# The inverse root mean square of a state-space group: one power on GpSimd in place of Newton steps on VectorE

## The chip, the cores and the metric

The kernel runs on one core of a Trainium2 chip. The metric is device time in microseconds, the median of several runs; lower is better. The engines are TensorE (PE in the profile, PEld its weight loads), VectorE (DVE), ScalarE (ACT), GpSimd (POOL) and SyncE (SP, which issues DMAs). Each engine works through its own queue in order, and semaphores hold it where it needs another engine's result.

## The reference

Two layers of a decoder trunk on 512 tokens of width 1024, in float32. A layer is a half-step SwiGLU feed-forward block, a mixer and a second half-step feed-forward block, each behind a root-mean-square normalization. The mixer has two branches, stick-breaking attention (4 heads) and a Mamba-2 state-space scan (24 heads in 8 groups), merged by gates. What the change touches is the end of the state-space branch, the normalization of each group of 192 channels:

```python
y = y.reshape(b, s, SSM_D_INNER) * jax.nn.silu(z.astype(jnp.float32))
yg = y.reshape(b, s, SSM_GROUPS, SSM_D_INNER // SSM_GROUPS)
yg = yg * lax.rsqrt(jnp.mean(yg * yg, axis=-1, keepdims=True) + NORM_EPS)
return (yg.reshape(b, s, SSM_D_INNER) * ssm_norm.astype(jnp.float32)).astype(z.dtype)
```

## The kernel before

Activations are held transposed, channels on partitions and 512 tokens along the free axis. Dense products are done in three matmuls per block of 128 rows: weights and activations are each split into a high part of reduced precision and a low part, and high x high, high x low and low x high are summed (`mm3`, lines 315 to 317). Every weight block comes from memory through `wraw`, ScalarE makes the high part (`whi`, line 282) and VectorE the low one (`wlo`, line 284).

The order of all queues is written out by the program itself. The dense products are the backbone. Everything else is a side task, a Python generator that is put on a list (`spawn`) and advanced by one step at each tick; a tick comes after each three matmuls of the backbone (`dense` calls `tick`), and `yield n` lets a task rest for n ticks. So a number after `yield` decides how many steps of the backbone stand ahead of the task's next instructions in each queue; it is no time and no wait.

In the mixer the backbone is the input projection, and three kinds of side tasks run beside it:

- `conv_block`: the causal convolution of one projected block of 128 channels. ScalarE applies the first tap (line 1024), VectorE three more (line 1027), ScalarE the tanh (line 1032), VectorE the product (line 1039), and for x and B blocks TensorE transposes the result (line 853, into `pt`).
- `ssd_group`: the scan of one group over four chunks of 128 tokens, one group after the other (`ssd_on`). GpSimd weights the inputs (lines 1137, 1139), masks the decay (1145) and forms products (1147, 1179, 1184); ScalarE forms the decays and, per chunk, the sum of squares of the gated output (line 1189, into a column of `ss`). When the four sums are there, the group is normalized: `ss`, 128 tokens x 4 chunks, is scaled and shifted (line 1209), `rsqrt_small` writes the inverse root to `rstd` (tile `gny`), VectorE multiplies the first 128 channels by it (line 1219), ScalarE the remaining 64 (line 1221, four instructions into `acc`), and TensorE transposes them back some ticks later.
- attention and the gates, which are not touched.

`rsqrt_small` starts from the bit trick (line 491: the bits of the number, as an integer, times -0.5, plus a constant) and refines it by three Newton steps of three instructions each (lines 493 to 495), all on VectorE and all on 128x4.

Of the kernel before, what the change touches and what calls it, by code (L numbers as in the profile page):

```python
# [8 lines left out]
F32 = mybir.dt.float32  # L9
F32R = mybir.dt.float32r  # L10
I32 = mybir.dt.int32
AF = mybir.ActivationFunctionType
ALU = mybir.AluOpType
# [4 lines left out]
P = 128  # L18
SEQ = 512
NT = SEQ // P  # L20
# [9 lines left out]
GW = HPG * HD  # L30
# [6 lines left out]
EPS = 1e-6  # L37
# [126 lines left out]
class Builder:  # L164
# [298 lines left out]
    def consts(self):  # L463
        nc = self.nc
        c = self.cst
        self.ident = c.tile([P, P], F32, name="ident")
        make_identity(nc, self.ident)
        self.ones = c.tile([P, P], F32, name="ones")
        nc.vector.memset(self.ones, 1.0)
        self.eps = c.tile([P, 1], F32, name="eps")  # L470
        nc.vector.memset(self.eps, EPS)
        self.nones = c.tile([P, P], F32R, name="nones")
        self.ntri = c.tile([P, P], F32R, name="ntri")
        with self.tc.tile_pool(name="cst_tmp", bufs=1, reuse_waits="tile") as tp:
            neg = tp.tile([P, P], F32, name="neg")
            nc.vector.memset(neg, -1.0)
            nc.vector.tensor_copy(self.nones, neg)
            tri = tp.tile([P, P], F32, name="tri")
            nc.gpsimd.affine_select(out=tri, in_=neg, pattern=[[-1, P]], compare_op=ALU.is_ge, fill=0.0,
                                    base=0, channel_multiplier=1)  # L480
            nc.vector.tensor_copy(self.ntri, tri)
        self.upto = c.tile([P, P], F32, name="upto")
        nc.gpsimd.affine_select(out=self.upto, in_=self.ones, pattern=[[1, P]], compare_op=ALU.is_ge, fill=0.0,
                                base=0, channel_multiplier=-1)


    def rsqrt_small(self, v, y):

        eng = self.nc.vector
        t = self.t(self.mp, v.shape, "gnt", bufs=1)  # L490
        eng.tensor_scalar(y.bitcast(I32), v.bitcast(I32), -0.5, 1597463007.0, op0=ALU.mult, op1=ALU.add)
        for _ in range(3):
            eng.scalar_tensor_tensor(t, y, -0.5, v, op0=ALU.mult, op1=ALU.mult)
            eng.tensor_tensor(t, t, y, op=ALU.mult)
            eng.scalar_tensor_tensor(y, t, 1.5, y, op0=ALU.add, op1=ALU.mult)

    def norm_start(self):
        self.h, self.diff = [None] * KB, [None] * KB
# [605 lines left out]
    def ssd_group(self, layer, g):  # L1104
        nc, mp, tok = self.nc, self.mp, None
# [9 lines left out]
        y = self.t(mp, [P, NT, GW], "y", bufs=1)  # L1115
        ss = self.t(mp, [P, NT], "ss")
# [89 lines left out]
            yield 1  # L1206
        self.give("xs")
        yield 1
        nc.vector.tensor_scalar(ss, ss, 1.0 / GW, EPS, op0=ALU.mult, op1=ALU.add)
        rstd = self.t(mp, [P, NT], "gny")  # L1210
        self.rsqrt_small(ss, rstd)
        yield 2
        if g % 2 == 0:
            self.tail = self.t(self.nrm, [P, NT, P], "acc")
        tail = self.tail
# [319 lines left out]
```

## Time and profile before

| | |
|---|---|
| median of three runs | 2582.1 us (2581.85 to 2583.41) |
| the profiled execution, its own time | 2582.94 us |
| its span, first to last instruction | 2581.2 us |
| granted TensorE clock | 0.999 |
| TensorE busy | 2559.8 us |
| VectorE busy | 1752.4 us |
| ScalarE busy | 1282.0 us |
| GpSimd busy | 498.5 us |
| each of the eleven instructions on 128x4 | 0.16 to 0.20 us, 16 times or 48 times |

A row of a table of groups reads: line, engine, operation, written tile <- read tiles, shape, count, then busy time in us and mean in ns of one, then the engine's idle time before it and who ended it. A row of the table of waits reads: engine, tile and line that waited <- engine, tile and line that ended the wait: us in total, times, longest. A row of a timeline reads: start, length, engine, line, operation, tiles, shapes, count and, in brackets, the idle time before it with its releaser. A row about one line or tile gives the shortest, median and longest duration in ns and the first and last start. The chain of waits follows the work that ended last, each piece with start and length.

### The profile page before, as it was taken

Reading aid. Unit: us, or ns where it says so; the run is one execution under the profiler, and the core shown is the slowest. Engines: PE = TensorE matmul, PEld = TensorE weight load, DVE = VectorE, ACT = ScalarE, POOL = GpSimd, SP = SyncE. Lnnn points to the kernel's source line nnn. Section 1 sums busy time; section 2 is a strip of 40 time slices with the busy share of each in tenths; the row PEclk is TensorE's granted clock in tenths of the full one; section 3 lists DMA queues with packets and bytes.
Section 4 is the critical chain, followed back from the end, with each engine's and each line's share of the span. In section 5 each row is a group of like instructions: output and inputs, shape, how many; then the busy total and the mean of one; then the engine's idle time right before and its main releaser. Section 6 shows DMA issues by size and latency. Waiting matters only on the chain.

```text
span 2581.2 us, 38169 instructions
## 1 busy us (share of the span) xinstructions
PE 2559.8 (99%) x15028; PEld 2288.4 (89%) x15028; DVE 1752.4 (68%) x2426; ACT 1282.0 (50%) x2103; POOL 498.5 (19%) x614
## 2 busy tenths in 40 slices
PE   9999999999999999999999999999999999999998
PEld 7898988888888889899998989888888888899997
DVE  8575875676664478586885858756676644876766
ACT  6343556665554255343653535566555533543444
POOL 0121201143341002121121312012333310022120
PEclk9999999999999999999999999999999999999999
DMA  6454542233333454545364545423333334455452
GB/s 183 138 159 136 132 138 87 99 103 110 101 105 107 139 162 139 164 139 164 106 180 139 156 141 136 139 72 111 99 103 104 116 109 143 152 143 168 142 162 78
DMA packets 104659, 335.76 MB, mean 130 GB/s; under 512 B 11872, under 2 KB 15392, under 8 KB 104480
## 3 DMA queue, kind: packets, MB, share of 16 engines
q1 hardware_dynamic: 92672, 292.84, 34.2%
q0 software_dynamic: 10944, 39.85, 8.6%
q8 instruction: 118, 1.93, 0.3%
q10 hardware_dynamic: 864, 0.64, 0.1%
q14 instruction: 61, 0.50, 0.1%
HBM read 320.60 MB, written 12.68 MB: 129 GB/s over the span
## 4 chain that ended last, share of the span: by engine, by line
PE 93%; DVE 4%; ACT 2%; issue 1%; DMA 0%; POOL 0%; SPq 0%; DVEq 0%; ACTq 0%
PE mm L315 26%; PE mm L317 25%; PE mm L316 25%; PE pa L316 3%; PE pa L317 3%; PE pa L315 3%; PE pa L1169 2%; DVE wlo L284 1%; PE pa L1171 1%; PE pt L853 1%; PE pt L1154 1%; DVE cv L1027 1%; PE pt L1152 1%; ACT whi L282 1%; PE pa L453 0%
## 5 line engine op out<-in xcount | busy, mean ns | idle before, releaser
L282 ACT CAST whi<-wraw 128x1024 fp32r<-128x1024 f32 (+3 forms) x440 | 435.1, 989 | 584.9 <-PE mm L317 485.0
L284 DVE TENSOR_TENSOR wlo<-wraw,whi 128x1024 fp32r<-128x1024 f32 (+3 forms) x440 | 538.7, 1224 | 165.9 <-ACT whi L282 164.5
L315 PE MATMUL mm<-hhi,whi 128*128 128x512 f32 (+1 forms) x1584 | 565.1, 357 | 0.0
L317 PE MATMUL mm<-hlo,whi 128*128 128x512 f32 (+1 forms) x1584 | 554.1, 350 | 0.4 <-DVE hlo L507 0.4
L316 PE MATMUL mm<-hhi,wlo 128*128 128x512 f32 (+1 forms) x1584 | 553.0, 349 | 0.0
L317 PEld LDWEIGHTS mm<-hlo,whi 128*128 128x128 f32 x1584 | 299.9, 189 | 40.3 <-DVE hlo L507 0.8
L316 PEld LDWEIGHTS mm<-hhi,wlo 128*128 128x128 f32 x1584 | 300.4, 190 | 34.6 <-DVE wlo L284 0.2
L315 PEld LDWEIGHTS mm<-hhi,whi 128*128 128x128 f32 x1584 | 300.3, 190 | 34.2 <-ACT hhi L505 0.4
L284 DVE TENSOR_TENSOR wlo<-s,whi 128x1024 fp32r<-128x1024 f32 x152 | 235.2, 1561 | 60.4 <-ACT whi L282 60.4
L315 PE MATMUL mm<-act,whi 128*128 128x512 f32 (+1 forms) x710 | 274.2, 386 | 0.0
L317 PE MATMUL mm<-act,whi 128*128 128x512 f32 (+1 forms) x710 | 274.2, 386 | 0.0
L316 PE MATMUL mm<-act,wlo 128*128 128x512 f32 (+1 forms) x710 | 274.1, 386 | 0.0
L315 PE MATMUL mm<-th,whi 128*128 128x256 f32 x912 | 257.4, 282 | 0.0
L317 PE MATMUL mm<-tl,whi 128*128 128x256 f32 x912 | 257.0, 282 | 0.0
L316 PE MATMUL mm<-th,wlo 128*128 128x256 f32 x912 | 256.9, 282 | 0.0
L626 POOL TENSOR_TENSOR g<-g,rs 128x512 f32<-128x512 f32 x76 | 132.5, 1744 | 553.4 <-DVE g L633 534.3
L282 ACT CAST whi<-s 128x1024 fp32r<-128x1024 f32 x152 | 159.3, 1048 | 102.4 <-PE mm L317 60.7
L652 DVE SCALAR_TENSOR_TENSOR x<-mm,x 128x512 f32<-128x512 f32 x93 | 64.1, 689 | 196.0 <-PE mm L317 196.0
L254 POOL DMA_DIRECT2D s<-in_wflat_dram x76 | 65.6, 863 | 621.3 <-DMA s<-in_wflat_dram 332.4
L315 PEld LDWEIGHTS mm<-th,whi 128*128 128x128 f32 x912 | 172.4, 189 | 0.0
L316 PEld LDWEIGHTS mm<-th,wlo 128*128 128x128 f32 x912 | 172.0, 189 | 0.0
L317 PEld LDWEIGHTS mm<-tl,whi 128*128 128x128 f32 x912 | 171.9, 188 | 0.0
(306 smaller groups left out, 5088.9 us busy)
## 6 DMA issues: line engine op xcount, KB each, us to landing
wraw<-in_wflat_dram SPq DMA_DIRECT2D x328, 512.0 KB, 3.6
s<-in_wflat_dram SPq DMA_DIRECT2D x76, 512.0 KB, 4.7
s<-in_wflat_dram POOLq DMA_DIRECT2D x76, 512.0 KB, 7.4
wraw<-in_wflat_dram SPq DMA_DIRECT2D x88, 384.0 KB, 3.1
cumb<-cum_d SPq DMA_DIRECT2D x16, 768.0 KB, 4.8
xd<-x SPq DMA_DIRECT2D x16, 256.0 KB, 3.2
wraw<-in_wflat_dram SPq DMA_DIRECT2D x16, 256.0 KB, 3.6
x<-xd SPq DMA_DIRECT2D x16, 256.0 KB, 3.9
```

The lines of the kernel that those rows point to most:

```text
L254: self.nc.gpsimd.dma_start(raw, src, accum_op=ALU.add)
L282: nc.scalar.copy(hi[:, :n], raw[:, :n])
L284: nc.vector.tensor_tensor(lo[:, :n], raw[:, :n], hi[:, :n].bitcast(F32), op=ALU.subtract)
L315: mm(ps, a[0], b[0], start=start, stop=False, **kw)
L316: mm(ps, a[1], b[0], start=False, stop=False, **kw)
L317: mm(ps, a[0], b[1], start=False, stop=stop, **kw)
L626: eng.tensor_tensor(r, r, self.rs[:, cols].unsqueeze(1).to_broadcast([P, 2, half]), op=ALU.mult)
L652: self.nc.vector.scalar_tensor_tensor(x, pd, 0.5, x, op0=ALU.mult, op1=ALU.add)
L853: self.nc.tensor.transpose(pt[:, cs], src[:, cs], self.ident)
L1027: nc.vector.scalar_tensor_tensor(u[:, j:], ps[:, :SEQ - j], tap[KCONV - 1 - j], u[:, j:], op0=ALU.mult, op1=ALU.add)
L1152: nc.tensor.matmul(pc[:, :P], bt[:, span(c)], ct[:, span(c)], start=True, stop=True)
L1169: nc.tensor.matmul(py[:, i * HD:(i + 1) * HD], decs[c][:, i, :], xdts[c][:, i, :], start=True, stop=True)
```

## The change

The scale and shift of `ss` moves from VectorE to GpSimd. The inverse root is one GpSimd instruction, `ss` to the power of a constant tile that holds -0.5. The bit trick and the Newton steps go, with their temporary tile. The task then rests three ticks and not two. The constant's memset is added at the start, in a tile shared with `eps`. Lines after line 487 are eight less in the changed kernel.

```diff
-        self.eps = c.tile([P, 1], F32, name="eps")
+        small = c.tile([P, 1 + NT], F32, name="small")
+        self.eps, self.root = small[:, :1], small[:, 1:]
         nc.vector.memset(self.eps, EPS)
+        nc.vector.memset(self.root, -0.5)
...
-    def rsqrt_small(self, v, y):
-
-        eng = self.nc.vector
-        t = self.t(self.mp, v.shape, "gnt", bufs=1)
-        eng.tensor_scalar(y.bitcast(I32), v.bitcast(I32), -0.5, 1597463007.0, op0=ALU.mult, op1=ALU.add)
-        for _ in range(3):
-            eng.scalar_tensor_tensor(t, y, -0.5, v, op0=ALU.mult, op1=ALU.mult)
-            eng.tensor_tensor(t, t, y, op=ALU.mult)
-            eng.scalar_tensor_tensor(y, t, 1.5, y, op0=ALU.add, op1=ALU.mult)
...
         self.give("xs")
         yield 1
-        nc.vector.tensor_scalar(ss, ss, 1.0 / GW, EPS, op0=ALU.mult, op1=ALU.add)
         rstd = self.t(mp, [P, NT], "gny")
-        self.rsqrt_small(ss, rstd)
-        yield 2
+        nc.gpsimd.tensor_scalar(ss, ss, 1.0 / GW, EPS, op0=ALU.mult, op1=ALU.add)
+        nc.gpsimd.tensor_tensor(rstd, ss, self.root, op=ALU.pow)
+        yield 3
```

VectorE's queue at the end of group 2 of the first layer, before (`cv_5856` is a convolution block, `wlo` a low weight part, `raw_5896` the normalized group):

```order
L1027 SCALAR_TENSOR_TENSOR cv_5856<-mm_5790,conv_4136,cv_5856 128x511
L284 TENSOR_TENSOR wlo_5859<-wraw_5718,whi_5858 128x1024
L1209 TENSOR_SCALAR ss_5589<-ss_5589 128x4
L491 TENSOR_SCALAR gny_5875<-ss_5589 128x4
...
L495 SCALAR_TENSOR_TENSOR gny_5875<-gnt_5876,gny_5875 128x4
L1027 SCALAR_TENSOR_TENSOR cv_5856<-mm_5790,conv_4136,cv_5856 128x510
L1027 SCALAR_TENSOR_TENSOR cv_5856<-mm_5790,conv_4136,cv_5856 128x509
L1219 TENSOR_TENSOR raw_5896<-y_5588,gny_5875 128x512
L1039 SCALAR_TENSOR_TENSOR cv_5856<-raw_5855,cv_5856 128x512
```

And the same place of the changed kernel:

```order
L1019 SCALAR_TENSOR_TENSOR cv_5837<-mm_5771,conv_4137,cv_5837 128x511
L284 TENSOR_TENSOR wlo_5840<-wraw_5699,whi_5839 128x1024
L1019 SCALAR_TENSOR_TENSOR cv_5837<-mm_5771,conv_4137,cv_5837 128x510
L1019 SCALAR_TENSOR_TENSOR cv_5837<-mm_5771,conv_4137,cv_5837 128x509
L1211 TENSOR_TENSOR raw_5870<-y_5569,gny_5855 128x512
L1031 SCALAR_TENSOR_TENSOR cv_5837<-raw_5836,cv_5837 128x512
```

The eleven instructions between the weight part and the second tap are gone; the normalization still stands ahead of the convolution's product.

GpSimd's queue at the same place of the changed kernel (`xw` and `xdt` are the next group's weighted inputs):

```order
L1171 TENSOR_TENSOR y_5569<-y_5569,t_969_5823 128x192
L1176 TENSOR_TENSOR y_5569<-y_5569,z_5781 128x192
L1202 TENSOR_SCALAR ss_5570<-ss_5570 128x4
L1203 TENSOR_TENSOR gny_5855<-ss_5570,small 128x4
L1129 TENSOR_TENSOR xw_6034<-xs_5563,sq_4398 128x192
L1131 TENSOR_TENSOR xdt_6036<-xs_5563,sq_4398 128x192
```

Before, the product (now line 1176) was followed at once by the next group's `xw`; the two new instructions stand between them. ScalarE's queue is the same at this place, with the four scalings by `gny` ahead of the convolution's tanh:

```order
L282 CAST whi_5839<-wraw_5699 128x1024
L1181 ACTIVATE t_976_5845,ss_5570<-y_5569 128x192
L1213 ACTIVATE acc_5869<-y_5569,gny_5855 128x64 x4
L1024 ACTIVATE raw_5836<-cv_5837 128x512
L1016 ACTIVATE cv_5888<-mm_5830,conv_4137 128x512
```

TensorE's matmuls are the same in number; some transposes of normalized groups and first products of groups stand one step of the backbone (three matmuls) later.

## The prediction

> **What bounds the kernel now.** I read the busy shares first, then what TensorE waits for, then the chain of waits around those waits.
>
> ```profile
> PE 2559.8 (99%) x15028; PEld 2288.4 (89%) x15028; DVE 1752.4 (68%) x2426; ACT 1282.0 (50%) x2103; POOL 498.5 (19%) x614
> PE pt L853 <- DVE cv L1039: 4.7, 8, 0.8
> PE pt L853 <- DVE cv L1039: 1.6, 3, 0.5
> PE pt L853 <- DVE cv L1039: 0.8, 1, 0.8
> PE pt L853 <- DVE cv L1039: 0.7, 1, 0.7
> ACT acc L1221 <- DVE gny L495: 18.0, 6, 3.0
> ```
>
> TensorE is busy for 2559.8 of 2581.2 us, so only a wait of TensorE can be won; the 29 us of VectorE work that the change removes are worth nothing by themselves. The second row is its longest entry in the table of waits: eight times the transposes of line 853 wait for the convolution's last step. The third is that table for 600 to 775 us alone: three of the eight lie there, and the same row comes out, 1.6 us and three times, for 1880 to 2055 us. The last says that six times ScalarE's scaling of the tail (line 1221) waits 3.0 us for the end of the Newton chain: in groups 2, 4 and 6 of both layers, and these are the six places where TensorE stalls. The other two of the eight are the fourth and fifth row, the table for 505 to 510 us and for 1784 to 1790 us (the same place of the second layer, 1279 us later, as 1880 is to 601). No group has come to its root there: the first normalization starts at 538.6 us (row of line 1219 below). They stay.
>
> The chain of waits between 595 and 612 us, group 2 of the first layer (start, length, what):
>
> ```profile
> 600.76 0.66 issue
> 601.42 1.04 ACT whi L282
> 602.48 1.23 DVE wlo L284
> 603.71 0.09 DVE ss L1209
> 603.82 0.18 DVE gny L491
> 604.03 0.17 DVE gnt L493
> ...
> 605.60 0.16 DVE gny L495
> 605.76 0.67 DVE cv L1027
> 606.46 0.76 DVE cv L1027
> 607.25 0.04 issue
> 607.30 0.64 ACT raw L1032
> 607.96 0.70 DVE cv L1039
> 608.67 0.04 issue
> 608.71 0.66 PE pt L853 x4
> ```
>
> All eleven small instructions, 603.71 to 605.76 us, stand on the path to the transposes, and nothing in the convolution needs them: they only stand in front of its second and third tap in VectorE's queue. What the stall costs is read from TensorE's timeline there:
>
> ```profile
> 607.56 0.39 PE L316 MATMUL mm<-hhi,wlo 128*128 128x512 f32 x1
> 607.79 0.39 PE L317 MATMUL mm<-hlo,whi 128*128 128x512 f32 x1
> 608.71 0.66 PE L853 MATMUL pt<-ident,cv 128*128 128x128 f32 x4 [0.53 <-DVE cv L1039]
> ```
>
> Matmuls follow each other at 0.23 us; the transposes start 0.92 us after the last one. So 0.69 us is lost, and without a wait they would start at 608.02.
>
> **The change, part by part.** Removed from VectorE in each of 16 groups: the scale and shift (line 1209), the bit trick (491) and nine Newton steps.
>
> ```profile
> L495 DVE SCALAR_TENSOR_TENSOR gny<-gnt,gny 128x4 f32<-128x4 f32 x48 | 7.8, 163 | 1.6
> L1209 DVE TENSOR_SCALAR ss<-ss 128x4 f32<-128x4 f32 x16 | 3.2, 198 | 6.6 <-ACT t L1189 6.6
> ```
>
> Eleven instructions at about 0.16 us and one start each 0.2 us make 2.1 us (603.63 to 605.76), and 29 us of busy time in 16 groups (11 x 0.163 x 16). Of that only the part that TensorE sees counts. In group 2 the convolution's two taps would follow wlo at once, 603.71 + 0.67 + 0.76 = 605.14, against 607.22 now. From there 0.64 (line 1032) and 0.70 (1039) give about 606.6 at the transposes, which are due at 608.02: a spare 1.4 us, if nothing else holds them.
>
> Something else can: ScalarE's order is unchanged, so the four tail scalings (1.07 us) still stand ahead of the tanh of line 1032, and they need the power.
>
> ```profile
> 602.62 0.19 ACT L1189 ACTIVATION_READ_ACCUMULATOR t<-y 128x1 f32 x1
> 605.80 1.07 ACT L1221 ACTIVATE acc<-y,gny 128x64 f32<-128x64 f32 x4 [2.99 <-DVE gny L495]
> 607.30 0.63 ACT L1032 ACTIVATE raw<-cv 128x512 f32<-128x512 f32 x1 [0.43 <-DVE cv L1027]
> ```
>
> Added on GpSimd: a scale and shift, and a power, each on 128x4. If the power is written at X, the transposes can start at X + 1.07 + 0.63 + 0.70 and some 0.15 for four hand-overs, X + 2.55. So X up to 605.47 gives the whole 0.69 us, X of 606.16 gives nothing, and later ones cost 1 us for each us. The multiplication of line 1219 needs the power as well, and the convolution's last step stands behind it in VectorE's queue; it takes 0.68 us and runs beside the tails and the tanh, so it is never the later of the two.
>
> When can GpSimd begin? The sum of squares is complete at 602.81. GpSimd is then idle: its last product ended at 600.72 and its next instruction came at 610.11.
>
> ```profile
> 595.71 1.23 DVE L284 TENSOR_TENSOR wlo<-wraw,whi 128x1024 fp32r<-128x1024 f32 x1
> 595.89 1.50 POOL L1184 TENSOR_TENSOR y<-y,z 128x192 f32<-128x192 f32 x1
> 600.12 0.60 POOL L1184 TENSOR_TENSOR y<-y,z 128x192 f32<-128x192 f32 x1
> 610.11 1.06 POOL L1137 TENSOR_TENSOR xw<-xs,sq 128x192 f32<-128x192 f32 x1 [9.39 <-ACT xs L1053]
> ```
>
> But the same product takes 1.50 instead of 0.60 us where VectorE forms wlo beside it, as if it stood still until that ended. In group 2 wlo runs from 602.48 to 603.71. So I let GpSimd start at 603.71 and not at 602.85. The Trainium skill says so too (GPSIMD Engine Reference, section 8, Key points): GpSimd shares its SBUF interfaces with VectorE, in contention with VectorE instructions that have two SBUF inputs, as wlo's subtraction has. By that rule the power has 0.86 us less room than without it, and the pair of rows above agrees.
>
> What two such instructions cost, no row shows. The nearest:
>
> ```profile
> L1139 POOL TENSOR_TENSOR xdt<-xs,sq x64: 506/512/1228, 511.0 to 2073.9; 128x192 f32<-128x192 f32 x64
> L626 POOL TENSOR_TENSOR c<-c,rs x38: 1280/1281/1292, 88.1 to 2529.7; 128x512 f32<-128x512 f32 x38
> L626 DVE TENSOR_TENSOR g<-g,rs x38: 691/691/693, 91.1 to 2532.5; 128x512 f32<-128x512 f32 x38
> ```
>
> GpSimd's binary operation takes 0.51 us on 192 columns and 1.28 on 512: 2.4 ns a column and some 0.05 us. At four columns that is 0.06 us; I take 0.2 for the scale and shift, a little over what VectorE needs. The power, D, has 0.2 us as its lower bound. Its upper bound is ten arithmetic steps, as many as the chain that it replaces, each at the 0.51 us of the 192-column operation: 5.1 us. I take 0.8. The chain's 2 us on VectorE are almost all fixed cost, paid ten times for four columns; inside one instruction that is paid once, and ten steps of 2.4 ns on four columns are 0.1 us. A logarithm and an exponential may need several times as many. So X = 603.71 + 0.2 + 0.8 = 604.7, which is 0.76 us ahead of the limit. The whole gain holds up to D = 1.55, break-even is D = 2.25.
>
> The Trainium skill speaks against the step (GPSIMD Engine Reference, section 4.1, Engine selection): elementwise arithmetic belongs on VectorE, GpSimd is about two times slower. The last two rows, 1.28 against 0.69 us for the same shape, agree. By that rule the two instructions would cost twice two of VectorE's, about 0.65 us: still less than the eleven, and the sum stays.
>
> Sum: 6 x 0.69 = 4.1 us off the path.
>
> At nothing I put the following. Groups 0, 1, 3, 5 and 7 show no wait of TensorE now. In group 0 the power stands ahead of the next group's products in GpSimd's queue, which now start at 535.55, while the operation behind them waits until 541.68 for ScalarE; some 5 us of cover.
>
> ```profile
> 535.55 0.51 POOL L1137 TENSOR_TENSOR xw<-xs,sq 128x192 f32<-128x192 f32 x1
> 541.68 0.52 POOL L1145 TENSOR_SCALAR_AFFINE_SELECT dec<-dec 128x384 f32<-128x384 f32 x1 [5.15 <-ACT dec L1143]
> L1219 DVE TENSOR_TENSOR raw<-y,gny x16: 680/685/693, 538.6 to 2088.4; 128x512 f32<-128x512 f32 x16
> 543.46 0.44 PE pa L853 x4
> ```
>
> In other groups GpSimd waits for data there, as in the row at 610.11. The wait of three ticks instead of two puts the normalization one step (three matmuls, 0.68 us) later in the queues, and a few transposes with it; TensorE's number of matmuls is the same, and in group 0 the transposes (543.46) come 4 us after their operand is ready (538.6 + 0.69), as the last two rows show. Were this cover gone, it would cost what a late power costs, below. The extra memset at the start lies beside the first loads.
>
> The profiled execution took 2582.94 us (span 2581.2 and 1.7 around it); less 4.1 it is 2578.8. It lies 0.8 over the median of the runs, 2582.1, which gives 2578.0. After that the places at 507 and 1786 us, where attention and the first blocks fill VectorE, are the only waits of this kind left.
>
> **Rivals.** What a measurement of this kernel can tell from no change is about 0.2%, 5.2 us; the whole of the forecast lies inside that.
>
> A: the wait changes its owner. With D between 1.55 and 3.1 the tails wait for GpSimd as they now wait for VectorE: at D = 1.9 half the gain is left (2580), at 2.25 nothing (2582), at 3.1 six times 0.85 is lost (2587). For it: the tails wait 3.0 us today and the power has only 0.76 us to spare. Against it: four columns are little for any engine.
>
> B, slower: the power is computed in software, step by step, and D is over 3.1. Then ScalarE stands at the tails with the tanh, the next tap and the next weight block behind it, and TensorE's transposes wait in the six groups. At the upper bound, 5.1, X is 609.0, the transposes start at 611.56 instead of 608.71, and six times 2.85 makes 17 us: 2599. It decides from D = 3.1 on. For it: no row shows a power on this engine. Against it: the price per column in the rows.
>
> C: the stalls go and the time falls by more than 5.2 us. The six waits give 4.1 and the next two are out of reach, so this needs another microsecond, from the spread of the runs (2581.85 to 2583.41 now) or from the shifted order: about 2576.5.
>
> D: the stalls stay, because the first taps or the weight block in front (601.42 to 603.71) hold them. Then 2582. The 1.4 us of room counted above speak against it.
>
> **Chances.** Forecast, within 0.2%: 0.53. A: 0.13. B: 0.18. C: 0.12. D: 0.04. So faster by over 0.2% is 0.12, slower 0.18, the same 0.70. The time is that of the forecast, 2578. The range goes from 2576.5 to 2590: it leaves out half of C and the part of B with D over 3.6, some 0.06 and 0.13.
>
> **What would show it.** Right: the row of line 853 waiting for the convolution (853 and 1039 here) falls from eight times to two; the chain of waits runs on TensorE through these places; the power's row has a mean under 1.5 us; VectorE's busy time falls by some 29 us. Wrong: a power of several microseconds, ScalarE's tail waiting for GpSimd by more than 3 us, and TensorE still waiting six times for the convolution; or new waits of TensorE at groups 0, 1, 3, 5 or 7.

## The result and the profile after

The changed kernel takes 2577.65 us (2577.19 to 2579.32, 20 runs), the kernel before 2582.1 us (2581.73 to 2583.89, 20 runs): 4.45 us less, a ratio of 0.9982 with a 95% interval of 0.9976 to 0.9988. That is within the 0.2% that the prediction counts as the same, though a ratio of 1 lies outside the interval, and 0.35 us from the predicted 2578.0.

Busy shares of the changed kernel, then its longest waits of TensorE and one of ScalarE from the tables of waits:

```profile
PE 2558.2 (99%) x15028; PEld 2288.4 (89%) x15028; DVE 1724.0 (67%) x2251; ACT 1280.6 (50%) x2103; POOL 522.1 (20%) x646
PE pt L845 <- DVE cv L1031: 1.5, 2, 0.8
PE pa L958 <- DVE y L408: 1.3, 4, 0.5
ACT acc L1213 <- POOL gny L1203: 12.5, 6, 2.1
```

VectorE does 28.4 us less, GpSimd 23.6 us more. TensorE waits for the convolution twice where it waited eight times. ScalarE still waits six times for the root, now of GpSimd and 2.1 us each in place of 3.0; TensorE does not wait behind it.

The two new instructions, from the rows of their tile and line (shortest, median and longest in ns):

```profile
L1203 POOL TENSOR_TENSOR gny<-ss,small x16: 1017/1017/1043, 535.7 to 2081.3; 128x4 f32<-128x4 f32 x16
L1202 POOL TENSOR_SCALAR ss<-ss x16: 192/194/870, 535.4 to 2081.0; 128x4 f32<-128x4 f32 x16
```

And group 2 of the first layer, from the timelines of VectorE, ScalarE, GpSimd and TensorE:

```profile
601.70 1.23 DVE L284 TENSOR_TENSOR wlo<-wraw,whi 128x1024 fp32r<-128x1024 f32 x1 [0.18 <-ACT whi L282]
602.84 1.53 DVE L1019 SCALAR_TENSOR_TENSOR cv<-mm,conv,cv 128x510 f32<-128x510 f32 x2
604.28 0.68 DVE L1211 TENSOR_TENSOR raw<-y,gny 128x512 f32<-128x512 f32 x1
605.73 0.69 DVE L1031 SCALAR_TENSOR_TENSOR cv<-raw,cv 128x512 f32<-128x512 f32 x1 [0.76 <-ACT raw L1024]
...
601.83 0.19 ACT L1181 ACTIVATION_READ_ACCUMULATOR t<-y 128x1 f32 x1
604.11 1.07 ACT L1213 ACTIVATE acc<-y,gny 128x64 f32<-128x64 f32 x4 [2.09 <-POOL gny L1203]
605.08 0.62 ACT L1024 ACTIVATE raw<-cv 128x512 f32<-128x512 f32 x1
...
602.11 0.87 POOL L1202 TENSOR_SCALAR ss<-ss 128x4 f32<-128x4 f32 x1 [2.17 <-ACT t L1181]
603.06 1.02 POOL L1203 TENSOR_TENSOR gny<-ss,small 128x4 f32<-128x4 f32 x1
...
607.00 0.39 PE L317 MATMUL mm<-hlo,whi 128*128 128x512 f32 x1
607.23 0.60 PE L845 MATMUL pt<-ident,cv 128*128 128x128 f32 x4
607.59 0.47 PE L315 MATMUL mm<-hhi,whi 128*128 128x512 f32 x1
```

The two taps follow the weight part at once (602.84). The transposes start 0.23 us after the matmul before them, without a wait, and their operand is ready at 606.42, so 0.81 us of room is left. The chain between power and transposes is the one that limits it now: power to 604.08, scalings to 605.18, tanh to 605.70, last step to 606.42.

Where the time went: laid beside each other matmul by matmul (15028 in both traces), the kernel before falls behind by 0.74 to 0.77 us at each of the six places, about 4.5 us together. The rest of the difference between the two profiled spans, 5.2 us, is some 0.8 us of the first 30 us; the start varies that much without a change of the kernel (below, e11).

### The profile page after: what moved, and what is told of

Read it like the earlier page. It is cut to its first block, busy times and chain, and to the rows that moved or that the text cites. A ratio compares the mean times of both kernels' runs of the same rounds, so it can differ in the third digit from the quotient of the medians.

```text
span 2576.0 us, 38026 instructions
## 1 busy us (share of the span) xinstructions
PE 2558.2 (99%) x15028; PEld 2288.4 (89%) x15028; DVE 1724.0 (67%) x2251; ACT 1280.6 (50%) x2103; POOL 522.1 (20%) x646
## 4 chain that ended last, share of the span: by engine, by line
PE 94%; DVE 3%; ACT 2%; issue 0%; DMA 0%; POOL 0%; SPq 0%; DVEq 0%; ACTq 0%
PE mm L315 26%; PE mm L317 26%; PE mm L316 26%; PE pa L316 3%; PE pa L317 3%; PE pa L315 3%; PE pa L1161 2%; DVE wlo L284 1%; PE pa L1163 1%; PE pt L1146 1%; PE pt L845 1%; PE pt L1144 1%; PE pa L845 0%; PE pa L453 0%; PE pa L960 0%
```

## The experiments

**Is it the engine or the later place?** The change does two things: it takes the root off VectorE, and it lets the task rest three ticks, which moves normalizations and transposes in the queues. Each was done alone. TensorE's instructions stand in the first run as in the changed kernel, in the second as in the kernel before.

```diff
 # e1, from the kernel before
         self.rsqrt_small(ss, rstd)
-        yield 2
+        yield 3
 # e2, from the changed kernel
         nc.gpsimd.tensor_tensor(rstd, ss, self.root, op=ALU.pow)
-        yield 3
+        yield 2
```

> The kernel before with the rest of three ticks alone; the root stays on VectorE, and the matmuls stand in the order of the changed kernel. Theory (the gain is six waits of TensorE, which end because the eleven instructions no longer stand ahead of the convolution's taps in VectorE's queue): nothing gained, 2582.1 within 1 us, eight waits for the convolution. Rival (the later place of the normalization makes the gain): 2577.7 and two waits.

> The changed kernel with the rest of two ticks again; the power stays on GpSimd, and the matmuls stand in the order of the kernel before. Theory: the whole gain, 2577.7 within 1 us, two waits for the convolution. Rival (the later place makes it): 2582.

Measured: e1 2582.16 us against 2582.35 for the kernel before on the same chip, ratio 1.0 (0.9991 to 1.0009); e2 2577.74, ratio 0.9982 (0.9973 to 0.9991). The waits of TensorE in e1 and then in e2:

```profile
PE pt L853 <- DVE cv L1039: 4.7, 8, 0.7
```

```profile
PE pt L845 <- DVE cv L1031: 1.5, 2, 0.8
```

The whole gain comes with the engine, none with the tick; the third tick is not needed.

**Is it the length of VectorE's chain, or what replaces it?** In e3 nothing goes to GpSimd; two of three Newton steps are left out, so the root is less exact.

```diff
 # e3, from the kernel before
-        for _ in range(3):
+        for _ in range(1):
```

> The kernel before with one Newton step in place of three: two steps are left out, and the root is less exact. VectorE's chain is 6 x 0.197 = 1.18 us shorter in each group; nothing goes to GpSimd. Theory: 1.18 is more than the 0.69 of each wait, so the six waits end and the time is that of the changed kernel, 2577.9 within 1 us, with VectorE's busy time 16 us lower. Rival (what VectorE saves counts in proportion, 96 of 176 instructions): 2579.7. Rival (it takes GpSimd's power): 2582.

Measured: 2577.65 us, ratio 0.9982 (0.9974 to 0.9991), two waits for the convolution, VectorE busy 1737.8 us:

```profile
PE 2558.0 (99%) x15028; PEld 2288.6 (89%) x15028; DVE 1737.8 (67%) x2330; ACT 1282.4 (50%) x2103; POOL 496.1 (19%) x614
```

VectorE saves half of what the change saves, and the time falls by the same amount. So a wait is paid, not work: 1.18 us less ahead of the taps brings as much as the whole 2.1. How little would do was not tried; by the prediction's sum it is the 0.69 of the wait.

**How late may the power be?** One and then three more powers ahead of the one that is used; their results are not used.

```diff
 # e4 with range(1), e5 with range(3), from the changed kernel
         nc.gpsimd.tensor_scalar(ss, ss, 1.0 / GW, EPS, op0=ALU.mult, op1=ALU.add)
+        spare = self.t(mp, [P, NT], "gnt", bufs=1)
+        for _ in range(1):
+            nc.gpsimd.tensor_tensor(spare, ss, self.root, op=ALU.pow)
         nc.gpsimd.tensor_tensor(rstd, ss, self.root, op=ALU.pow)
```

> The changed kernel with one more power of 1.02 us ahead of the one that is used. In the changed kernel the operand of the transposes is ready at 606.42 us and they start at 607.39, so 0.97 us of room. Theory: the second power takes 1.05 with its start, so 0.1 us of wait in six groups, 2578.3. By the break-even of the prediction (power's length 2.25; here 2.07) half a microsecond of each wait would be back, 2581. Rival (the gain is the earlier root): all of it lost, 2582 or more.

> The changed kernel with three more powers ahead of the one that is used: the root comes 3.05 us later than in the changed kernel (a power takes 1.02). Theory (past its room of 0.77 us, which the run with two powers shows, a late power costs TensorE as much as it is late, in the six groups): 6 x 2.3 = 14 us, and up to 2 x 2.3 more in group 1 of each layer, where that run shows a first wait: 2591 to 2597, slower than before. By the break-even of the prediction (2.25, then 1 us for each us in six groups): 2593. Rival (the waits are taken up by the slack of other queues): 2582 or less.

Measured: e4 2580.53 us, ratio 0.9992 (0.9983 to 1.0001): by the medians nearly two thirds of the gain lost. e5 2603.45 us, ratio 1.0085 (1.0069 to 1.01): 21 us slower than before. From e4's chain of waits in group 2 and its timeline of TensorE:

```profile
603.87 0.88 POOL ss L1202
...
604.82 1.02 POOL gnt L1205
605.84 1.00 POOL gny L1206
...
607.12 0.81 ACT acc L1216 x3
607.93 0.53 ACT raw L1024
...
608.48 0.70 DVE cv L1031
```

```profile
608.77 0.39 PE L317 MATMUL mm<-hlo,whi 128*128 128x512 f32 x1
609.23 0.66 PE L845 MATMUL pt<-ident,cv 128*128 128x128 f32 x4
```

The powers now stand on the path with ScalarE's scalings behind them: the wait has a new owner. Both expectations missed. For e4 the room had been read as 0.97 us, from the chain of waits, where the piece begins at 607.39, after the modelled end of the matmul before it; the timeline has the transposes at 607.23, which makes 0.81. The power that is used starts 0.99 us after the added one (605.81 and 604.82 in GpSimd's timeline), 0.18 more than the room, and 0.05 pass between the operand and the transposes: they come 0.46 us after the matmul before them in place of 0.23, at all six places. e4's table of waits does not show this. It lists two waits for the convolution, as in the changed kernel, because it counts from the modelled end of a matmul, 0.39 us after its start, while the next one can start after 0.23; a wait this short falls out of the table. Another 0.26 was lost in group 1 of each layer. Matched matmul by matmul and without the first 30 us, e4 is 2.3 us behind the changed kernel, about half of the gain. The medians are 2.9 apart; the starts of the two profiled executions differ by 1.4, and whether the rest of the 2.9 lies there in the other executions was not read.

For e5 the transposes come 2.39 us late at each of the six places, 14.3 in all, as expected; the other 10 us are in places where nothing waited before. From its waits of TensorE, and from the rows of the root's tile VectorE's multiplication and its wait:

```profile
PE pt L845 <- DVE cv L1031: 15.9, 10, 2.2
PE pa L1161 <- DVE dec L1152: 2.4, 2, 1.2
...
PE pt L845 <- DVE bT L1031: 0.8, 2, 0.4
```

```profile
L1214 DVE TENSOR_TENSOR raw<-y,gny x16: 691/693/998, 539.9 to 2110.5; 128x512 f32<-128x512 f32 x16
  DVE raw L1214: 58.7, 16
```

VectorE's multiplication now waits for the power in all 16 groups, 3.7 us each (last row: us in all, count), and what stands behind it in VectorE's queue, the next decay and the next taps, comes late for TensorE in some of the other groups. How the 10 us are shared out among these places was not followed further. A root that is late by d us costs nothing in the six groups up to d = 0.81, and about d - 0.81 in each of them beyond; at 1 us (e4) group 1 of each layer loses a little too, and at 3 us (e5) other groups together lose nearly as much as the six.

**What does a power cost?** Unused powers and products at the start of the program, on 0.75.

```diff
 # e8, from the changed kernel
+        probe, made = self.tt[6], self.tt[7]
+        nc.gpsimd.memset(probe, 0.75)
+        for n in (4, 4, 16, 64, 256):
+            nc.gpsimd.tensor_tensor(made[:, :n], probe[:, :n], probe[:, :n], op=ALU.pow)
+        for n in (4, 64, 256):
+            nc.gpsimd.tensor_tensor(made[:, :n], probe[:, :n], probe[:, :n], op=ALU.mult)
         self.norm_start()
```

> The changed kernel with powers of 128x4 (twice), 128x16, 128x64 and 128x256 and products of 128x4, 128x64 and 128x256 on GpSimd at the start, none of them used. If a power's 1.02 us is a fixed price, 128x256 takes little over it plus a product's 0.6; if it is the work on four columns, 0.2 us a column or so, 128x256 takes over 40 us. The products should take 0.06 to 0.7 us (2.4 ns a column and 0.05). The time of the whole means nothing here, since the powers may hold up the first loads on the same queue.

From the table of groups (line 1409 the powers, 1411 the products; busy us, mean ns of one):

```profile
L1409 POOL TENSOR_TENSOR tl<-tl 128x256 f32<-128x256 f32 x1 | 41.1, 41127 | 0.1
L1409 POOL TENSOR_TENSOR tl<-tl 128x64 f32<-128x64 f32 x1 | 10.8, 10815 | 0.1
L1409 POOL TENSOR_TENSOR tl<-tl 128x16 f32<-128x16 f32 x1 | 2.9, 2896 | 0.1
L1409 POOL TENSOR_TENSOR tl<-tl 128x4 f32<-128x4 f32 x2 | 2.1, 1026 | 0.2
L1411 POOL TENSOR_TENSOR tl<-tl 128x256 f32<-128x256 f32 x1 | 0.6, 612 | 0.1
...
L1411 POOL TENSOR_TENSOR tl<-tl 128x4 f32<-128x4 f32 x1 | 0.2, 200 | 0.1
```

(41127 - 1026) / 252 makes 0.159 us a column for a power, and some 0.39 us fixed; (612 - 200) / 252 makes 1.6 ns for a product. The product here multiplies a tile by itself, and its line does not reach further: the case's own product on 512 columns takes 1.28 us where it would give 1.0. A power of 256 columns costs 67 times a product of the same size. At four columns it is cheap because there are four.

**Can the same be had at the other two places?** At 507 and 1786 us VectorE's queue holds four gate products (0.56 us each) between the taps, and GpSimd is idle. GpSimd takes two instructions for each. e7 moved the first two, e9 the last three, e10 the middle two.

```diff
 # from the changed kernel; c < 2 in e7, c > 0 in e9, c in (1, 2) in e10
-            nc.vector.scalar_tensor_tensor(z, r[:, :2 * GW], 1.0, z, op0=ALU.add, op1=ALU.mult)
+            if c < 2:
+                nc.gpsimd.tensor_scalar(r[:, :2 * GW], r[:, :2 * GW], 1.0, None, op0=ALU.add)
+                nc.gpsimd.tensor_tensor(z, r[:, :2 * GW], z, op=ALU.mult)
+            else:
+                nc.vector.scalar_tensor_tensor(z, r[:, :2 * GW], 1.0, z, op0=ALU.add, op1=ALU.mult)
```

> The changed kernel, and at the other two waits for the convolution (507 and 1786 us) two of the four gate products that VectorE forms there, 0.56 us each, go to GpSimd as two instructions each, which is idle there. Theory (work that stands in VectorE's queue ahead of a transpose that TensorE waits for is worth its length, up to the wait of 0.92 us): 0.6 to 0.9 us less at each of two places, 2576.0 to 2576.5. Rival (ScalarE's tanh, which needs the buffers that GpSimd then holds, takes over the wait): 2577.7 or more.

> As the run with two gate products on GpSimd, but the second, third and fourth of them and not the first two. The first one's buffer is the one that the fourth tanh needs; kept on VectorE it is free again before that. Theory (the fault there was the buffer, not the idea): VectorE then has 1.5 us less ahead of the transposes, the wait of 0.92 us at 507 and 1786 us ends or falls under 0.2, and the time is 1.4 to 1.9 us under the changed kernel, about 2576. Rival (any work on GpSimd here comes back as a wait, since each product takes 2.2 us there against 0.56): 2577.7 or more.

> The same with the second and third gate product alone on GpSimd; 1.0 us less ahead of the transposes on VectorE. Theory: the wait of 0.92 us falls to 0.1 to 0.4 at the two places, 1.0 to 1.6 us under the changed kernel, about 2576.4. Rival: 2577.7 or more.

> The changed kernel itself, on the same chip as the two runs beside it, as the mark that they are measured against: 2577.7 within 0.5 us, two waits for the convolution. How much of the difference to the kernel before lies in the first 20 us is read from this profile too: the theory expects that part to vary from run to run by up to 1 us, whatever the kernel.

Measured: e7 2579.12 us; and side by side e9 2578.12, e10 2579.04 and the changed kernel (e11) 2578.07. Nothing gained, in all three: e9 stands level with the changed kernel, and matched matmul by matmul e7 and e10 lose 0.7 us at each of the two places. In e7 the rival was right: ScalarE's fourth tanh waits for the buffer that GpSimd still holds, and the next weight block behind it is late (its timeline):

```profile
503.47 1.01 POOL L1080 TENSOR_TENSOR z<-raw,z 128x384 f32<-128x384 f32 x1
504.52 0.53 ACT L1076 ACTIVATE raw<-z 128x384 f32<-128x384 f32 x1 [1.58 <-POOL z L1080]
```

In e9 that buffer is free and VectorE comes to the convolution's last step 0.6 us earlier (505.68, in the changed kernel 506.27), but there the step itself takes twice its time. Its row over the whole program, then the place, from the timelines of VectorE and GpSimd:

```profile
L1031 DVE SCALAR_TENSOR_TENSOR cv<-raw,cv x24: 679/693/1495, 498.1 to 2043.8; 128x512 f32<-128x512 f32 x24
```

```profile
501.92 2.18 DVE L1019 SCALAR_TENSOR_TENSOR cv<-mm,conv,cv 128x510 f32<-128x510 f32 x3
...
505.68 1.50 DVE L1031 SCALAR_TENSOR_TENSOR cv<-raw,cv 128x512 f32<-128x512 f32 x1
...
501.91 1.19 POOL L1079 TENSOR_SCALAR raw<-raw 128x384 f32<-128x384 f32 x1 [14.30 <-ACT raw L1076]
503.19 1.02 POOL L1080 TENSOR_TENSOR z<-raw,z 128x384 f32<-128x384 f32 x1
...
505.43 1.20 POOL L1080 TENSOR_TENSOR z<-raw,z 128x384 f32<-128x384 f32 x1
```

1.50 us in place of 0.69, beside a GpSimd product. The three taps beside GpSimd's work from 501.9 on, its product at 503.19 among it, run at their ordinary 0.73: they read one operand from PSUM, the last step reads both from SBUF. VectorE's part of e10 shows the same, a gate product of 1.27 in place of 0.56 and a last step of 1.48 us. So in e9 and e10 the expectation of a gain fell, not because the waited-for work had a different price on the path, but because the moved work slows what stays. The theory of e9, that only the buffer was at fault in e7, was wrong. No version here beats the changed kernel.

e11 also answers for the start. It is the same program as the changed kernel; its span is 2577.6 us against 2576.0, and matched matmul by matmul it is 1.68 us behind at 11.7 us and 1.64 at the end. TensorE's first wait for activations and two pairs of its first matmuls, e11 and then the changed kernel's first profile:

```profile
PE pa L453 <- ACT hhi L497: 0.7, 1, 0.7
...
8.28 1.05 PE L453 MATMUL pa<-hhi,whi 128*128 128x512 f32 x2
9.13 1.05 PE L453 MATMUL pa<-hhi,wlo 128*128 128x512 f32 x2
```

```profile
PE pa L453 <- ACT hhi L497: 0.3, 1, 0.3
...
8.47 0.62 PE L453 MATMUL pa<-hlo,whi 128*128 128x512 f32 x2
8.92 0.62 PE L453 MATMUL pa<-hhi,whi 128*128 128x512 f32 x2
```

The later first wait makes 0.3 of the 1.7 us. The rest is pace: in e11 pairs of matmuls follow each other at 0.85 us until 10 us, in the other profile at 0.46 from 8 us on. The traces do not show what slows them; the granted clock reads 1.00 in both. So the first 12 us varied by 1.7 us with the kernel unchanged, more than the 1 us that was expected, and one or two microseconds between two single executions say nothing of a change.

## Why the prediction was right

**The reading of the bound** held. Of eight waits of TensorE for the convolution the six behind the Newton chain ended, the two at 507 and 1786 us stayed, and no group without a wait got one. The prediction's first sign, that row's fall from eight to two, would not have been enough alone: e4's row falls as far with half of the gain lost. e3 shows what the prediction assumed, that the 29 us of work do not count by themselves.

**The sum** was 6 x 0.69 = 4.1 us; the traces show 0.74 to 0.77 at each place, and the medians are 4.45 apart. What the sum lacked is that transposes that come late also take a little longer. From their start to the next matmul it is 0.41 us in the kernel before (608.71 to the row here) and 0.35 in the changed one (607.23 to 607.59):

```profile
609.12 0.48 PE L315 MATMUL mm<-hhi,whi 128*128 128x512 f32 x1
```

It is so at all six places, and six times 0.06 is the missing 0.4. Behind the late transposes of e4 and e5 it is 0.41 as well, so this part does not grow with the wait (0.23 us late in e4, 2.39 in e5). Why it is so stays open.

**The start on GpSimd** was put at the end of the weight part, not at the end of the sum of squares. It is so: the scale and shift takes 0.87 us in the six groups where the weight part runs and 0.19 in the ten others, four of them beside a tap of the convolution; in group 2 it ends at 602.98, 0.05 us after the weight part. The Trainium skill's sentence on the shared interfaces (GPSIMD Engine Reference, section 8, Key points) names contention with VectorE instructions that have two SBUF inputs. That is borne out here, and e9 bears it out the other way round: there VectorE's last step took 1.50 in place of 0.69 us.

**The power's length** was taken as 0.8 us and is 1.02, within the whole-gain limit of 1.55. But the argument for 0.8 was wrong: it took the columns to cost next to nothing and the price to be fixed. By e8 0.64 of the 1.02 us are the four columns. With 32 columns the same argument would have given 1.5 us, against 5.5 by e8's line. The upper bound, ten steps at 0.51 us, was no bound of the mechanism either. That 0.8 came near and the bound held is luck: the tile has four columns. The line of 2.4 ns a column and 0.05 us was too low there too: 0.06 us, where e8's product of four columns took 0.20. The Trainium skill's factor of two for elementwise arithmetic on GpSimd (GPSIMD Engine Reference, section 4.1, Engine selection) holds for a product here (1.28 against 0.69 us on 128x512) and is no guide to a power.

**The limits** in D were a whole gain up to 1.55 and break-even at 2.25. Read from e4 and the changed kernel, the whole gain lasts to 1.02 + 0.81 = 1.83, and at 2.0 a third of a wait is lost in the six groups. By the slope of 1 us for each us between e4 and e5, break-even at one of these places would be near 2.5; for the whole time it lies lower, since e4 and e5 lose in other groups too, and no run lies on it. The hand-overs were counted at 0.15 us and nearly vanish. On the other side the prediction let a late power cost only in six groups; e5, at a length of four powers, loses ten microseconds more in others. Its rival B would have been dearer than the 17 us given for 5.1: e5 is 21 us over the kernel before already at 4.1.

**The rivals.** A is the state of the changed kernel in form (ScalarE waits for GpSimd, 2.1 us, six times), with 0.81 us between it and TensorE; e4 pushes it over that edge. B, a root that comes too late by microseconds, was brought about by e5. C and D did not come: the gain stopped where the waits stopped.

## What to carry to other kernels

On a kernel whose TensorE is busy throughout, look for instructions that stand in front of a waited-for step in its queue without being needed by it; what their removal is worth is the wait that ends, not their length. Before work is given to an idle engine, ask three things: what that engine holds while it works (a buffer), whom it slows (here VectorE instructions with two SBUF operands), and how its price grows with the shape. A power on GpSimd is a good trade for a handful of columns and a ruinous one for a tile.

## What the runs showed of the hardware

- A power on GpSimd costs about 0.39 us and 0.159 us a column (1.03 us at 4, 2.90 at 16, 10.8 at 64, 41.1 at 256, e8; 1.02 at 4 in the changed kernel); a product of a tile by itself 0.20 us at 4 and 0.61 at 256.
- GpSimd and VectorE instructions with two SBUF operands hold each other up: a GpSimd scale and shift on 128x4 took 0.87 in place of 0.19 us beside VectorE's two-operand subtraction, and a VectorE step with two SBUF operands 1.50 in place of 0.69 us beside a GpSimd product (e9). VectorE steps with one operand in PSUM kept their 0.73 us beside GpSimd (e9).
- Four transposes that came late took 0.41 us to the next matmul, on time 0.35 (the kernel before, the changed kernel, e4 and e5).
- The first 12 us of the same program differed by 1.7 us between two executions (the changed kernel and e11).
